# Attention of a two-layer hybrid block: how the low-rank heads' operands are split, and where their products stand between the attention units

## The chip, the cores and the metric

One core of one Trainium2 chip. The metric is the device time of one execution in microseconds, the median of the runs. Lower is better.

## What is computed

Two layers over 512 latent tokens (and 256 context tokens, 768 together), model width 1024. Each layer is half a SwiGLU, a token mixing, half a SwiGLU. The token mixing has grouped-query heads, a short convolution and low-rank heads side by side:

```python
def mla_heads(p, g_cq, g_ckv, w_uq, w_ukv, g_qn, g_kn, g_qr, g_kr):
    cq, ckv, kr = jnp.split(p, [MLA_Q_LORA, MLA_Q_LORA + MLA_KV_LORA], axis=-1)
    q = (rms_norm(cq, g_cq) @ w_uq).reshape(b, s, MLA_HEADS, MLA_NOPE + MLA_ROPE).transpose(0, 2, 1, 3)
    kv = (rms_norm(ckv, g_ckv) @ w_ukv).reshape(b, s, MLA_HEADS, MLA_NOPE + MLA_V).transpose(0, 2, 1, 3)
    ...
def token_mixing(...):
    ya_l, ya_c = gqa_mix(...)      # 6 query heads, 2 key heads, 64 wide
    ym_l, ym_c = mla_mix(...)      # 6 low-rank heads, 64 + 32 wide
    y_l = jnp.concatenate([ya_l, short_conv(s_l, conv_w, conv_b), ym_l], axis=-1) @ w_out
```

In layer 0 both latent and context tokens are queries (`need_ctx`); in layer 1 only the latent tokens are. Everything is float32.

## The kernel before

The kernel is written with a tile framework that tracks data and buffers; its compiler pass sets each engine's order of instructions from the program order, the dependencies and the free buffers. `chain("te")` holds TensorE to the written order in the attention. There ScalarE, VectorE and GpSimd have no such chain.

Nearly every float32 matrix product is done with split operands: x = hi + lo, where hi is x rounded to the fast format (`fp32r`) and lo is x - hi, and hi*hi, hi*lo and lo*hi are summed in PSUM.

**The attention** (`attend`) goes through a list of units. A unit is one head and two blocks of 128 queries. In layer 0 a head has three units, two with latent queries against 768 keys and one with the context queries against 256 keys, so units n = 2, 5, 8, ... are short; heads 0 to 5 are grouped-query heads and 6 to 11 the low-rank ones, so the low-rank units start at n = 18. In layer 1 a head has two units, and low-rank units start at n = 12. In step n TensorE does, in this order: the first scores of unit n; the first transposes of unit n-1's probabilities; then, if there is a "mid" job, the second transposes of n-1, the job, the second scores of n, and otherwise the second scores and then the second transposes; the third transposes of n-1; the "b" jobs; the values product of unit n-2; the "end" jobs. VectorE takes the row maxima, ScalarE the exponentials, and the transposed probabilities are split from PSUM by ScalarE (hi) and VectorE (lo).

PSUM has two score buffers of two banks (`ps`), shared by scores and by the products `uq` and `ukv`, and four one-bank buffers (`po`) for transposes and values products. Between a scores product and the reuse of its buffer stand the maxima and the exponentials.

**The jobs** make the later heads' operands while earlier heads are attended to:

- `uq(t)`: queries of the low-rank heads for token tile t (18 matmuls of 288 columns into a `ps` buffer; ScalarE copies and squares, VectorE sums the squares).
- `ukv(t)`: keys and values of token tile t (12 matmuls of 384 columns into a `ps` buffer; ScalarE copies, squares and scales, VectorE subtracts from PSUM for the lo part of the values, GpSimd copies the shared rope part).
- `load_ukv(hf)`: one half of the weights of `ukv`, loaded and split.
- `queries(p)`: two more grouped-query heads transposed and split into hi and lo.
- `q_norm`, `k_norm(t0, t1)`: norm factors, put as a list of small VectorE operations on `side`; `trickle()` takes two of them at each of six places in a step, `trickle(100)` takes all that are left. After the factors stand the scalings: GpSimd for the queries (with rope) and for key tiles 0 to 3, VectorE for key tiles 4 and 5.
- `mla_part(hd, which, t0)`: up to four token tiles of one head's query (`which` 0) or key (1), transposed by TensorE into a `po` buffer, scaled by ScalarE into a temporary y; after the last group VectorE casts y to hi and GpSimd subtracts (line 1862) for lo.
- `mixnorm_a`, `mixnorm_b`: two finished heads are divided by their row sums.

`at(n, place, f)` and `up_at(n, f, t)` put a job into step n. Layer 0's step 0 begins at 729.5 us of the profiled execution, step 5 at 770.3, step 8 at 792.2, step 12 at 810.5, step 16 at 830.2, step 18 at 843.9; in layer 1 step 0 begins at 2171.7, step 8 at 2229.2, step 12 at 2253.9, step 14 at 2264.7, step 18 at 2288.0.

Of the kernel before, what the change touches and what calls it, by code (L numbers as in the profile page):

```python
# [9 lines left out]
F32R = mybir.dt.float32r  # L10
I32 = mybir.dt.int32
AF = mybir.ActivationFunctionType
ALU = mybir.AluOpType
AX = mybir.AxisListType

P = 128
# [4 lines left out]
T = SEQ + CTX  # L21
# [20 lines left out]
LAG = 1  # L42
LATE = {0: 1, 2: 1, 4: 1, 6: 1}
NATIVE = (0, 2)


@with_exitstack
def tile_net(ctx: ExitStack, tc: tile.TileContext, a, out):
# [34 lines left out]
    te, ve, se, pe = Engine(nc.tensor, "te"), Engine(nc.vector, "ve"), Engine(nc.scalar, "se"), nc.gpsimd  # L83

    const = ctx.enter_context(tc.tile_pool(name="const", bufs=1))
    pool = ctx.enter_context(tc.tile_pool(name="pool", bufs=1))
# [4 lines left out]
    def nm(s):  # L91
        uid[0] += 1
        return f"{s}{uid[0]}"

    def slot(dt=F32, w=T):
        return pool.tile([P, w], dt, name=nm("s"), tag="s", bufs=NSLOT)

    def temp(dt=F32, w=T):
        return pool.tile([P, w], dt, name=nm("t"), tag="t", bufs=NTMP)
# [10 lines left out]
    def f32(t):  # L110
        return t.bitcast(F32)
# [1170 lines left out]
    def trickle(n=2):  # L1282

        for _ in range(n):
            if side:
                side.pop(0)()
# [154 lines left out]
    def mixing(l, hin, early, streams, nxt, pre):  # L1441
        h, E, accs = hin
        need_ctx = streams[-1][0].stop == T
# [8 lines left out]
        g96 = cst("g96", l, [96, 2])  # L1452
# [5 lines left out]
        mix = [None] * 8  # L1458
# [37 lines left out]
        for c0, w, nt in ((0, 384, nqt), (384, 288, NT)):  # L1496
# [5 lines left out]
            for t in range(nt):  # L1502
# [21 lines left out]
                lo = 0 if t < nqt else 384  # L1524
# [72 lines left out]
        stats = {"ckv": Stats(ALL, 2 * P), "cq": Stats(slice(0, wq), 3 * P)}  # L1597
# [14 lines left out]
        for i in range(5):  # L1612
            name, g, w = ("ckv", gckv[:, i:i + 1], T) if i < 2 else ("cq", gcq[:, i - 2:i - 1], wq)
# [87 lines left out]
        def uq(t, between=()):  # L1701
            q = slot()
            q_tok.append(q)
            sq = temp()
            pt = ps().rearrange("p (f c) -> p f c", f=2)
            up([pt[:, f, :288] for f in range(2)], t, comp["cq"], 288, wuq, between)
            se.copy(q[:, :576].rearrange("p (f c) -> p f c", f=2), pt[:, :, :288])
            se.activation(out=sq[:, :576].rearrange("p (f c) -> p f c", f=2), in_=pt[:, :, :288], func=AF.Square)
            sv = sq[:, :576].rearrange("p (h d) -> p h d", d=96)

            def sums():
                ve.tensor_reduce(out=st3[:, t, 0:6], in_=sv[:, :, 0:64], axis=AX.X, op=ALU.add)
                ve.tensor_reduce(out=st3[:, t, 6:12], in_=sv[:, :, 64:96], axis=AX.X, op=ALU.add)
            return sums
# [14 lines left out]
        def ukv(t):  # L1729
            pt = ps()  # L1730
            up([pt[:, 512 * f:512 * f + 384] for f in range(2)], t, comp["ckv"], 384, wukv)
            if t != spill:
                k_tok.append(slot())
            v = slot(F32R)
            VM.append(v)
            pv = pt.rearrange("p (f x) -> p f x", f=2)
            vv = v.rearrange("p (f h s d) -> p f h s d", f=2, s=2, d=64)
            rk = rr["ckv"][:, t:t + 1]
            vp = pv[:, :, 192:384].rearrange("p f (h d) -> p f h d", d=64)
            if t == spill:  # L1740
                srcs = (pt[:, 0:128], pt[:, 128:896].rearrange("p (a b) -> p a b", b=384)[:, :, 0:64], pt[:, 576:704])
                for (kv, hs), src in zip(heads_of(t), srcs):
                    se.copy(kv[:, :, 0:64], src if len(src.shape) == 3 else src.rearrange("p (h d) -> p h d", d=64))
            else:
                kv = k_tok[t][:, :576].rearrange("p (f h d) -> p f h d", f=2, d=96)
                se.copy(kv[:, :, :, 0:64], pv[:, :, 0:192].rearrange("p f (h d) -> p f h d", d=64))
            for kv, hs in heads_of(t):
                pe.tensor_copy(kv[:, :, 64:96], bc(krr[:, t, :], 1, hs.stop - hs.start))
            sq = temp()
            se.activation(out=sq[:, :384].rearrange("p (f c) -> p f c", f=2), in_=pv[:, :, 0:192], func=AF.Square)  # L1750
            se.mul(vv[:, :, :, 0, :], vp, rk)
            ve.scalar_tensor_tensor(out=vv[:, :, :, 1, :], in0=vp, scalar=rk, in1=f32(v).rearrange(
                "p (f h s d) -> p f h s d", f=2, s=2, d=64)[:, :, :, 0, :], op0=ALU.mult, op1=ALU.subtract)
            return lambda: ve.tensor_reduce(out=st3[:, t, 12:18], in_=sq[:, :384].rearrange("p (h d) -> p h d", d=64), axis=AX.X,
                                            op=ALU.add)
# [82 lines left out]
        mla, ys = {}, {}  # L1838
# [4 lines left out]
        def mla_part(hd, which, t0):  # L1843

            tok, n, w = ((query_of, nqt, wq), (key_of, NT, T))[which]
            if t0 == 0:
                ys[hd, which] = temp()
            y = ys[hd, which]
            tp = po()
            m = min(4, n - t0)  # L1850
            for t in range(m):
                te.transpose(out=tp[:96, t * P:(t + 1) * P], in_=tok(t0 + t, hd), identity=ident)
            se.mul(y[:96, t0 * P:(t0 + m) * P], tp[:96, :m * P], g96[:, which:which + 1])
            if t0 + m < n:
                return
            if which == 0:
                hi = pool.tile([P, T], F32R, name=nm("qh"), tag="wh", bufs=3)
                lo = pool.tile([P, T], F32R, name=nm("ql"), tag="wl", bufs=3)
            else:
                hi, lo = slot(F32R), slot(F32R)  # L1860
            ve.tensor_copy(hi[:96, :w], y[:96, :w])
            pe.tensor_sub(lo[:96, :w], y[:96, :w], f32(hi)[:96, :w])
            mla[hd, which] = hi[:96, :], lo[:96, :]

        def mla_unit(hd):
# [5 lines left out]
        def at(n, place, f, *args):  # L1871
            jobs.setdefault((n, place), []).append(lambda: f(*args))

        def up_at(n, f, t):
            def start():
                jobs.setdefault((n, "end"), []).insert(0, f(t))
            at(n, "mid", start)

        per = 3 if need_ctx else 2
        up_at(0, lambda t: uq(t, stats["cq"].count_steps(stats["cq"].acc)), 1)  # L1880
        at(0, "end", lambda: uq(2)())
        at(1, "b", lambda: stats["cq"].mean())
        up_at(1, uq, 3)
        if need_ctx:
            at(1, "end", lambda: uq(4)())
            at(1, "end", lambda: uq(5)())
        at(1, "end", load_ukv, 0)
        at(1, "end", load_ukv, 1)
        at(2, "end", queries, 1)
        at(2, "end", q_norm)  # L1890
        at(3, "end", queries, 2)
        for t, n in enumerate((4, 5, 6, 7, 9, 14) if need_ctx else (3, 4, 5, 6, 7, 8)):
            if t == 5 and need_ctx:
                at(n, "end", lambda: ukv(5)())
            else:
                up_at(n, ukv, t)
            if t == 3:
                at(n, "end", k_norm, 0, 4)
            elif t == 5:
                at(n, "end", k_norm, 4, 6)  # L1900
                at(n + 1, "b", trickle, 100)
        for hd in range(12):
            mk = (lambda hd=hd: gqa_unit(hd)) if hd < 6 else (lambda hd=hd: mla_unit(hd - 6))
            s = per * hd
            if 5 <= hd < 11:
                q, k = ((s - 1, s + 1) if hd == 5 else (s, s + 1)) if need_ctx else ((s - 1, s) if hd == 5 else (s, s))
                at(q, "b", mla_part, hd - 5, 0, 0)
                if nqt > 4:
                    at(q, "end", mla_part, hd - 5, 0, 4)
                at(k, "b" if k > q else "end", mla_part, hd - 5, 1, 0)  # L1910
                at(k, "end", mla_part, hd - 5, 1, 4)
            if hd >= 2 and hd % 2 == 0:
                i = hd // 2 - 1 if hd < 8 else hd // 2 + 1
                m = s + (2 if need_ctx else 1)
                at(m, "end", mixnorm_a, i)
                at(m + 1, "b", mixnorm_b, i, 0)
                if nqt > 4:
                    at(m + 1, "end", mixnorm_b, i, 4)
            for qbs in lat_units:
                units.append(Unit(qbs, ALL, list(range(NT)), mk))  # L1920
            if need_ctx:
                units.append(Unit((4, 5), CTXS, [4, 5], mk))
# [11 lines left out]
            nc.sync.dma_start(out=raw, in_=a["wo"][l, 0])  # L1934
            first_out.append(wsplit(raw, 1024))

        n0 = per * 11
        at(n0 - 1, "end", out_block)
        places = [(n0 + n, p) for n in range(4) for p in ("b", "end")]
        for i, (n, p) in zip((3, 4, 0, 1, 2, 5, 6), places):  # L1940
# [35 lines left out]
    def wm0_high(g):  # L1976
        if g in NATIVE:
            return
# [5 lines left out]
    def wm0_low(g, i):  # L1984
        if g in NATIVE:
            return
# [3 lines left out]
    def wm0_mm(g, k0=0, k1=KD):  # L1990
        if k0 == 0:
            pms[g] = ps()
        pm = pms[g]
        if g in NATIVE:
            for kk in range(k0, k1):
# [233 lines left out]
```

## Time and profile before

| | |
|---|---|
| median of 3 runs | 2744.41 us (2742.31 to 2748.45) |
| profiled execution, its own time | 2748.81 us |
| its span, first to last instruction | 2747.0 us |
| TensorE matmul busy | 2669.8 us, 97% |
| VectorE busy | 2038.7 us, 74% |
| ScalarE busy | 1145.5 us, 42% |
| GpSimd busy | 188.8 us, 7% |
| granted TensorE clock, mean | 0.993 |

The profile names an engine's instruction by its operation, the tile that it writes and those that it reads (`po<-ident,s`: a transpose into a `po` buffer), with the shapes. Nearly all VectorE, ScalarE and TensorE instructions pass through one helper and so have line 66; the tiles tell them apart: `t<-po,g` is `mla_part` on ScalarE, `qh<-t` its cast, `ql<-t,qh` and `s<-t,s` its subtraction on GpSimd. PE is TensorE, DVE is VectorE, ACT is ScalarE, POOL is GpSimd. In brackets behind a row stands how long the engine had been idle before it and which instruction ended that.

### The profile page before, as it was taken

The page shows a single profiled execution, that of the slowest core. Times are in us where ns is not written, and L with a number is a line of the kernel's source. Part 1 is how long each engine was busy: PE and PEld are TensorE (multiplying, and loading weights), DVE is VectorE, ACT ScalarE, POOL GpSimd, SP SyncE. Part 2 cuts the span into 40 slices and gives each one's busy share as a digit, 9 for nine tenths or more (in the row PEclk, how much of TensorE's full clock was granted, in tenths as well). Part 3 has the DMA queues.
Part 4 walks back from the last instruction along what each step waited for, and adds up shares of the span by engine and source line. Part 5 has one row for each costly group of instructions (what it writes and reads, how often), then busy time and mean ns, then how long its engine had stood idle before and what let it go on. Part 6 is the DMA issues. An engine that isn't in the chain of part 4 may idle for free. (4 is left out here: it accounts for less than half of the span.)

```text
span 2747.0 us, 40650 instructions
## 1 busy us (share of the span) xinstructions
PE 2669.8 (97%) x16088; PEld 2525.6 (92%) x16088; DVE 2038.7 (74%) x3475; ACT 1145.5 (42%) x1991; POOL 188.8 (7%) x248
## 2 busy tenths in 40 slices
PE   8999999999988999999999999999999999999999
PEld 5999999989888889999999999999998888888987
DVE  6856777777688887777777777777776788666655
ACT  5223333341477633333334433333343578444433
POOL 0000000001232200000000000000000233001110
PEclk9999999999999999999999999999999999999999
DMA  7313333233100321333333123333325101346543
GB/s 249 115 61 103 108 108 107 78 102 129 33 2 9 106 89 60 104 104 108 108 108 100 58 89 106 108 105 105 101 72 172 35 9 39 106 118 164 156 125 115
DMA packets 102927, 266.09 MB, mean 97 GB/s; under 512 B 12240, under 2 KB 41680, under 8 KB 102736
## 3 DMA queue, kind: packets, MB, share of 16 engines
q1 hardware_dynamic: 96112, 249.33, 27.4%
q0 software_dynamic: 6624, 14.16, 2.6%
q8 instruction: 127, 2.08, 0.3%
q14 instruction: 64, 0.52, 0.1%
HBM read 256.63 MB, written 2.10 MB: 94 GB/s over the span
## 5 line engine op out<-in xcount | busy, mean ns | idle before, releaser
L66 PE MATMUL ps<-s,wh 128*128 128x384 f32 (+2 forms) x4292 | 989.4, 340 | 6.9 <-ACT t L66 4.1
L66 PEld LDWEIGHTS ps<-s,wh 128*128 128x128 f32 x4292 | 743.6, 188 | 53.8 <-ACT t L66 5.2
L66 PE MATMUL po<-s,wh 128*128 128x384 f32 (+2 forms) x3164 | 768.6, 329 | 9.9 <-ACT t L66 9.3
L66 PE MATMUL ps<-s,wl 128*128 128x384 f32 (+2 forms) x2146 | 613.2, 338 | 0.9 <-DVE wl L66 0.8
L66 PEld LDWEIGHTS po<-s,wh 128*128 128x128 f32 x3164 | 553.2, 188 | 26.0 <-ACT t L66 12.4
L66 PE MATMUL po<-s,wl 128*128 128x384 f32 (+2 forms) x1582 | 519.2, 328 | 0.0
L66 PEld LDWEIGHTS ps<-s,wl 128*128 128x128 f32 x2146 | 387.0, 188 | 21.8 <-DVE wl L66 3.1
L66 PEld LDWEIGHTS po<-s,wl 128*128 128x128 f32 x1582 | 297.5, 188 | 6.2
L66 DVE SCALAR_TENSOR_TENSOR junk<-mr,sb 128x1024 fp8e4<-128x1024 f32 x224 | 273.7, 1222 | 14.4 <-DMA mr<-in_wm_dram 13.5
L66 DVE SCALAR_TENSOR_TENSOR xT<-ps,mod,xT 128x256 f32<-128x256 f32 (+1 forms) x360 | 198.7, 594 | 107.7 <-PE ps L66 105.9
L66 DVE TENSOR_TENSOR wl<-wr,wh 128x1024 fp32r<-128x1024 f32 (+3 forms) x179 | 192.2, 1076 | 114.5 <-ACT wh L66 114.3
L66 ACT CAST wh<-wr 128x1024 fp32r<-128x1024 f32 (+3 forms) x179 | 165.3, 927 | 203.1 <-PE ps L66 137.2
L66 ACT ACTIVATE t<-t 128x384 f32<-128x384 f32 (+1 forms) x142 | 70.9, 500 | 303.3 <-DVE t L66 303.3
L66 PE MATMUL po<-s,s 128*128 128x256 f32 (+3 forms) x1216 | 190.9, 307 | 6.0 <-DVE pl L66 2.0
L66 ACT COPY t<-po 128x384 f32<-128x384 f32 (+2 forms) x215 | 97.1, 452 | 225.1 <-PE po L66 223.1
L66 PEld LDWEIGHTS po<-s,s 128*128 128x128 f32 x1216 | 172.6, 189 | 13.3 <-DVE pl L66 2.5
L1526 POOL TENSOR_TENSOR t<-s 128x544 f32<-128x544 f32 (+1 forms) x12 | 13.0, 1095 | 1863.8 <-ACT s L66 1858.9
L66 DVE TENSOR_TENSOR s<-t,s 128x768 fp32r<-128x768 f32 (+3 forms) x144 | 104.3, 728 | 47.0 <-ACT s L66 46.4
L66 ACT CAST wh<-ws 128x1024 fp32r<-128x1024 f32 x71 | 74.8, 1054 | 146.5 <-PE ps L66 92.3
L66 ACT CAST s<-t 128x768 fp32r<-128x768 f32 (+3 forms) x144 | 92.9, 652 | 102.6 <-DVE t L66 102.5
L66 DVE TENSOR_TENSOR t<-po,t 128x384 f32<-128x384 f32 (+2 forms) x223 | 115.4, 523 | 27.3 <-ACT t L66 26.6
L66 PE MATMUL po<-s,w 128*128 128x384 f32 x636 | 119.9, 337 | 0.0
(198 smaller groups left out, 3413.0 us busy)
## 6 DMA issues: line engine op xcount, KB each, us to landing
mr<-in_wm_dram SPq DMA_DIRECT2D x128, 512.0 KB, 3.3
wr<-in_wg_dram SPq DMA_DIRECT2D x82, 512.0 KB, 3.2
wu<-in_wu_dram SPq DMA_DIRECT2D x71, 512.0 KB, 3.3
t<-in_wd_dram SPq DMA_DIRECT2D x80, 384.0 KB, 3.6
wr<-in_wiT_dram SPq DMA_DIRECT2D x22, 512.0 KB, 3.6
ws<-in_wu_dram POOLq DMA_DIRECT2D x36, 256.0 KB, 4.3
wr<-in_wu_dram SPq DMA_DIRECT2D x17, 512.0 KB, 3.3
wr<-in_wo_dram SPq DMA_DIRECT2D x14, 512.0 KB, 3.9
```

The lines of the kernel that those rows point to most:

```text
L66: f(*args, **kw)
L1526: pe.tensor_mul(sq[:, lo:544], x[:, lo:544], x[:, lo:544])
```

## The change

Two edits. The first is in `mla_part`: ScalarE writes the scaled group from PSUM as hi straight away, and VectorE makes lo from the same PSUM group; the temporary, VectorE's cast and GpSimd's subtraction are gone. For head 0 it also takes all that is left on `side` before its first group. The second puts the places of the jobs in a table `PLAN`, with other places than before:

| job | layer 0 before | layer 0 after | layer 1 before | layer 1 after |
|---|---|---|---|---|
| `uq` 3 | 1 mid | 1 mid | 1 mid | 1 end |
| `uq` 5 | 1 end | 2 mid | | |
| `queries` 1, 2 | 2, 3 end | 1, 5 end | 2, 3 end | 2, 4 end |
| `ukv` 0 to 5 | 4, 5, 6, 7, 9 mid, 14 end | 4 end, 5, 6, 8, 11, 12 mid | 3, 4, 5, 6, 7, 8 mid | 2 end, 4, 5, 7, 8, 8 mid |
| `k_norm` of tiles 0-3, 4-5 | 7, 14 end | 8, 12 end | 6, 8 end | 7, 8 end |
| all left on `side` | 15 b | 13 b | 9 b | 9 b |
| query, key of low-rank head 0 | 14, 16 | 13, 16 | 9, 10 | 9, 10 |
| query of heads 2, 4 | 21, 27 | 21, 27 | 14, 18 | 13, 17 |
| key of heads 2, 4 | 22, 28 | 22, 28 | 14, 18 end | 14, 18 b and end |

`uq` 1, 2 and 4, `load_ukv`, `q_norm`, the other heads' parts and `mixnorm` stay where they were.

```diff
         def mla_part(hd, which, t0):
 
             tok, n, w = ((query_of, nqt, wq), (key_of, NT, T))[which]
-            if t0 == 0:
-                ys[hd, which] = temp()
-            y = ys[hd, which]
+            if hd == 0:
+                trickle(100)
+            if t0 == 0 and which == 0:
+                ys[hd, which] = [pool.tile([P, T], F32R, name=nm("q" + p), tag="w" + p, bufs=3) for p in "hl"]
+            elif t0 == 0:
+                ys[hd, which] = slot(F32R), slot(F32R)
+            hi, lo = ys[hd, which]
             tp = po()
...
-            se.mul(y[:96, t0 * P:(t0 + m) * P], tp[:96, :m * P], g96[:, which:which + 1])
+            c, g = slice(t0 * P, (t0 + m) * P), g96[:, which:which + 1]
+            se.mul(hi[:96, c], tp[:96, :m * P], g)
+            ve.scalar_tensor_tensor(out=lo[:96, c], in0=tp[:96, :m * P], scalar=g, in1=f32(hi)[:96, c], op0=ALU.mult,
+                                    op1=ALU.subtract)
             if t0 + m < n:
                 return
-            if which == 0:
...
-            ve.tensor_copy(hi[:96, :w], y[:96, :w])
-            pe.tensor_sub(lo[:96, :w], y[:96, :w], f32(hi)[:96, :w])
...
+PLAN = {True: {'uq': [(0, 'mid'), (0, 'end'), (1, 'mid'), (1, 'end'), (2, 'mid')], 'load': 1, 'qs': (1, 5), 'qn': 2,
+  'ukv': [(4, 'end'), (5, 'mid'), (6, 'mid'), (8, 'mid'), (11, 'mid'), (12, 'mid')], 'first': (13, 16), 'even': (0, 1), 'odd': (0, 1), 'mix': 2, 'flush': None},
+  False: {'uq': [(0, 'mid'), (0, 'end'), (1, 'end')], 'load': 1, 'qs': (2, 4), 'qn': 2,
+  'ukv': [(2, 'end'), (4, 'mid'), (5, 'mid'), (7, 'mid'), (8, 'mid'), (8, 'mid')], 'first': (9, 10), 'even': (0, 0), 'odd': (-1, 0), 'mix': 1, 'flush': 9}}
...
+        for t, (n, p) in enumerate(plan["ukv"]):
+            place(n, p, ukv, t)
             if t == 3:
                 at(n, "end", k_norm, 0, 4)
             elif t == 5:
                 at(n, "end", k_norm, 4, 6)
-                at(n + 1, "b", trickle, 100)
+        if plan.get("flush") is not None:
+            at(plan["flush"], "b", trickle, 100)
```

More of the change, by code (lines that the diff above doesn't have):

```diff
@@ L44 @@
 NATIVE = (0, 2)
+PLAN = {True: {'uq': [(0, 'mid'), (0, 'end'), (1, 'mid'), (1, 'end'), (2, 'mid')], 'load': 1, 'qs': (1, 5), 'qn': 2, 'ukv': [(4, 'end'), (5, 'mid'), (6, 'mid'), (8, 'mid'), (11, 'mid'), (12, 'mid')], 'first': (13, 16), 'even': (0, 1), 'odd': (0, 1), 'mix': 2, 'flush': None}, False: {'uq': [(0, 'mid'), (0, 'end'), (1, 'end')], 'load': 1, 'qs': (2, 4), 'qn': 2, 'ukv': [(2, 'end'), (4, 'mid'), (5, 'mid'), (7, 'mid'), (8, 'mid'), (8, 'mid')], 'first': (9, 10), 'even': (0, 0), 'odd': (-1, 0), 'mix': 1, 'flush': 9}}
 @with_exitstack
@@ L1852, in mla_part @@
                 te.transpose(out=tp[:96, t * P:(t + 1) * P], in_=tok(t0 + t, hd), identity=ident)
-            se.mul(y[:96, t0 * P:(t0 + m) * P], tp[:96, :m * P], g96[:, which:which + 1])
+            c, g = slice(t0 * P, (t0 + m) * P), g96[:, which:which + 1]
+            se.mul(hi[:96, c], tp[:96, :m * P], g)
+            ve.scalar_tensor_tensor(out=lo[:96, c], in0=tp[:96, :m * P], scalar=g, in1=f32(hi)[:96, c], op0=ALU.mult,
+                                    op1=ALU.subtract)
             if t0 + m < n:
                 return
-            if which == 0:
[L1857 to L1860, printed above, removed]
-            ve.tensor_copy(hi[:96, :w], y[:96, :w])
-            pe.tensor_sub(lo[:96, :w], y[:96, :w], f32(hi)[:96, :w])
             mla[hd, which] = hi[:96, :], lo[:96, :]
@@ L1877, in up_at, with first, place @@
             at(n, "mid", start)
[L1879 to L1894, printed above, removed]
-            else:
-                up_at(n, ukv, t)
+        def first(hd):
+            return (3 if need_ctx else 2) * hd
+        plan = PLAN[need_ctx]
+        def place(n, p, f, t):
+            if p == "mid":
+                up_at(n, f, t)
+            else:
+                at(n, "end", lambda: f(t)())
+        for t, (n, p) in enumerate(plan["uq"]):
+            place(n, p, (lambda t: uq(t, stats["cq"].count_steps(stats["cq"].acc))) if t == 0 else uq, t + 1)
+        at(plan["uq"][0][0] + 1, "b", lambda: stats["cq"].mean())
+        at(plan["load"], "end", load_ukv, 0)
+        at(plan["load"], "end", load_ukv, 1)
+        for p, n in enumerate(plan["qs"]):
+            at(n, "end", queries, p + 1)
+        at(plan["qn"], "end", q_norm)
+        for t, (n, p) in enumerate(plan["ukv"]):
+            place(n, p, ukv, t)
             if t == 3:
@@ L1900, in mixing @@
                 at(n, "end", k_norm, 4, 6)
-                at(n + 1, "b", trickle, 100)
+        if plan.get("flush") is not None:
+            at(plan["flush"], "b", trickle, 100)
         for hd in range(12):
             mk = (lambda hd=hd: gqa_unit(hd)) if hd < 6 else (lambda hd=hd: mla_unit(hd - 6))
-            s = per * hd
+            s = first(hd)
             if 5 <= hd < 11:
-                q, k = ((s - 1, s + 1) if hd == 5 else (s, s + 1)) if need_ctx else ((s - 1, s) if hd == 5 else (s, s))
+                q, k = plan["first"] if hd == 5 else (s + d for d in plan["odd" if hd % 2 else "even"])
                 at(q, "b", mla_part, hd - 5, 0, 0)
@@ L1913, in mixing @@
                 i = hd // 2 - 1 if hd < 8 else hd // 2 + 1
-                m = s + (2 if need_ctx else 1)
+                m = s + plan["mix"]
                 at(m, "end", mixnorm_a, i)
@@ L1935, in out_block @@
             first_out.append(wsplit(raw, 1024))
-        n0 = per * 11
+        n0 = first(11)
         at(n0 - 1, "end", out_block)
```

## The prediction

> **What bounds the kernel now.** First the page: the span and the engines' shares.
>
> ```profile
> span 2747.0 us, 40650 instructions
> PE 2669.8 (97%) x16088; PEld 2525.6 (92%) x16088; DVE 2038.7 (74%) x3475; ACT 1145.5 (42%) x1991; POOL 188.8 (7%) x248
> ```
>
> TensorE bounds the kernel, and the change takes no matmul away. So it can win only TensorE's idle time and time at a low granted clock, and only in the attention. Second view: busy time by stretch, for the grouped-query and the low-rank part of layer 0 and the same two parts of layer 1.
>
> ```profile
> 724.00:845.00 121.00, 102.80 (x693) 95.83 (x692) 93.24 (x209) 85.68 (x194) 27.12 (x48) 0.93 0.02 7
> 845.00:934.00 89.00, 81.77 (x617) 75.56 (x616) 72.25 (x124) 77.66 (x174) 29.33 (x16) 1.00 0.06 19
> 2168.00:2246.00 78.00, 70.13 (x482) 65.17 (x480) 68.53 (x151) 59.64 (x127) 20.90 (x39) 0.98 0.03 8
> 2246.00:2326.00 80.00, 75.53 (x565) 70.00 (x564) 66.31 (x115) 67.21 (x145) 22.57 (x15) 1.00 0.06 20
> ```
>
> The columns are length, then PE, PEld, DVE, ACT and POOL busy, then the clock. TensorE is idle for 18.2, 7.2, 7.9 and 4.5 us, 37.8 us in all. VectorE is busy 77, 81, 88 and 83%: none of these stretches has one clear bound, a late VectorE instruction soon holds TensorE. Third view: TensorE's order of time, with the waits that the moved jobs touch.
>
> ```profile
> 754.18 0.39 PE L66 MATMUL ps<-k,s 128*128 128x256 f32 x1 [0.61 <-ACT t L66]
> 761.14 0.36 PE L66 MATMUL po<-ph,s 128*128 128x256 f32 x1 [1.42 <-DVE s L66]
> 770.26 0.39 PE L66 MATMUL ps<-k,s 128*128 128x256 f32 x1 [1.26 <-DVE s L66]
> 772.30 0.48 PE L66 MATMUL po<-ident,t 128*128 128x128 f32 x1 [1.42 <-ACT t L66]
> 792.15 0.35 PE L66 MATMUL ps<-k,s 128*128 128x256 f32 x1 [0.77 <-DVE s L66]
> 807.56 0.33 PE L66 MATMUL po<-ident,t 128*128 128x128 f32 x1 [1.68 <-ACT t L66]
> 827.40 0.50 PE L66 MATMUL ps<-s,s 128*128 128x512 f32 x1 [0.85 <-DVE s L66]
> 838.78 0.28 PE L66 MATMUL po<-ident,s 128*96 128x128 f32 x1 [3.11 <-DVE s L66]
> 2229.20 0.76 PE L66 MATMUL ps<-s,s 128*128 128x512 f32 x1 [2.12 <-DVE m L66]
> 2270.19 0.39 PE L66 MATMUL po<-s,s 128*128 128x256 f32 x1 [0.98 <-DVE pl L66]
> 2293.69 0.38 PE L66 MATMUL po<-s,s 128*128 128x256 f32 x1 [0.99 <-DVE pl L66]
> ```
>
> Last, the stretches around the three worst places, same columns.
>
> ```profile
> 768.00:780.00 12.00, 9.32 (x48) 8.85 (x47) 8.41 (x22) 6.56 (x17) 6.68 (x14) 0.72 0.00 1
> 834.00:843.00 9.00, 5.89 (x39) 5.70 (x38) 7.68 (x23) 6.57 (x17) 1.82 (x1) 0.83 0.17 55
> 2226.00:2236.00 10.00, 7.88 (x46) 7.42 (x45) 7.83 (x22) 4.74 (x11) 3.20 (x4) 0.83 0.01 2
> ```
>
> After such waits the clock falls. What that costs I take as the missing share of the clock times the busy time: 0.28 x 9.32 = 2.6 us, 0.17 x 5.89 = 1.0 us and 0.17 x 7.88 = 1.3 us.
>
> **The change, part by part.**
>
> *A. `uq` 5 to step 2 mid, first `queries` to step 1 end (layer 0).* The wait at 754.18 is for a score buffer that `uq` 5 had just filled; the one at 761.14 is a values product whose `po` buffer the split of the queries in step 2 still held. Both causes move: the query split runs one step earlier, where VectorE has no other backlog, and `uq` 5 stands between the two scores of a short unit, where its 18 matmuls cover the exponentials. Full value 2.03 us. The second half of the `ukv` weights reuses the buffer of `uq`'s weights, so its split now comes a step later; it is first needed by `ukv` 0 at the end of step 4, so I price that at nothing. I take -1.5.
>
> *B. `ukv` 0 to step 4 end, second `queries` to step 5 end.* The waits at 770.26 (a buffer that `ukv` 0 still held) and 772.30 (exponentials of step 4) come one behind the other at the start of step 5. At the end of step 4, `ukv` 0 stands just where the second wait was and covers it. But `ukv` 1 in step 5 then needs `ukv` 0's buffer sooner.
>
> ```profile
> L66 ACT COPY s<-ps 128x384 f32<-128x384 f32 x5 | 2.4, 482 | 4.8 <-PE ps L66 4.8
> L66 ACT ACTIVATE t<-ps 128x384 f32<-128x384 f32 x6 | 3.0, 502 | 0.0
> L66 ACT ACTIVATE s<-ps,m 128x384 fp32r<-128x384 f32 x6 | 3.5, 589 | 0.0
> L66 DVE SCALAR_TENSOR_TENSOR s<-ps,m,s 128x384 fp32r<-128x384 f32 x6 | 3.7, 612 | 0.0
> ```
>
> ```profile
> 780.85 0.60 PE L66 MATMUL po<-ident,t 128*128 128x128 f32 x4
> ```
>
> Emptying it takes 0.48 + 0.50 + 0.59 + 0.61 = 2.2 us; TensorE has only a short unit's first scores and eight transposes in between, some 1.2 us (twice the last row). So 1.0 us of wait returns, and with it I expect half of the clock loss (1.3). Full value 1.26 + 1.42 + 2.6 = 5.3; I take -3.0.
>
> *C. `ukv` 3 from step 7 to 8, `ukv` 4 from 9 to 11.* Step 7 has no cover any more, so step 8 starts as step 11 did before: 1.68 (807.56) in place of 0.77 (792.15), +0.9. Step 11 keeps its 1.68, as the job stands behind the first transposes there.
>
> *D. `ukv` 5 from step 14 to 12, first head's query from 14 to 13, all of `side` at 13.* The wait of 3.11 at 838.78 is the transposes of the first head's last key tiles, which VectorE had not scaled in time, and the one at 827.40 is for `ukv` 5's buffer. Both lose their cause: two to three steps lie between the scaling and its reader. The norm factors of `k_norm` now fall as a burst on step 13, before its maxima: 12 small operations of 0.16 and four scalings of 0.29 us, 3 us of VectorE, with the third transposes' splits queued behind:
>
> ```profile
> 836.84 0.16 DVE L66 SCALAR_TENSOR_TENSOR m<-m,m 128x12 f32<-128x12 f32 x1
> 838.08 1.17 DVE L66 TENSOR_TENSOR s<-s,m 128x384 f32<-128x384 f32 x4
> ```
>
> Full value 3.11 + 0.85 + 1.0 = 5.0; I take -4.0.
>
> *E. Layer 1: `ukv` one step later and the first `k_norm` from step 6 to 7.* The wait of 2.12 at 2229.20 has its root in a tiny operation:
>
> ```profile
> 2221.85 3.15 DVE L66 TENSOR_TENSOR m<-m 128x4 f32<-128x4 f32 x1
> 2224.06 0.94 POOL L1748 COPY s<-kr 128x192 f32<-128x192 f32 x3
> 2230.63 3.20 POOL L1797 TENSOR_TENSOR s<-s,m 128x384 f32<-128x384 f32 x4 [5.63 <-DVE m L66]
> ```
>
> The first `k_norm`'s opening product, 128x4, takes 3.15 us instead of some 0.16 (the row of 836.84), and ends when GpSimd's run of scalings and copies does, at 2225.0. One step later that run is over: -(2.12 + 1.3) = -3.4. [...] So I count 2.0 of it back and take -1.4. The other moves of `ukv` in layer 1 I set at zero: TensorE's 7.9 us of idle time in that stretch, less the 2.12, is spread over small waits, and two `ukv` in step 8 cover as much as they ask.
>
> *F. Layer 1: queries of heads 2 and 4 a step earlier.* At 2270.19 and 2293.69 (steps 14 and 18) transposes of `mixnorm` and of a query stand together ahead of the values product, and VectorE is late with the split. The query's four go to steps 13 and 17: full 1.97, I take -1.5.
>
> *G. `mla_part`.* Over both layers there are 24 head operands in 24 groups of 512 and 18 of 256 columns.
>
> ```profile
> L66 ACT ACTIVATE t<-po,g 96x512 f32<-96x512 f32 x24 | 16.6, 693 | 0.5
> L66 ACT ACTIVATE t<-po,g 96x256 f32<-96x256 f32 x18 | 8.5, 471 | 1.9 <-PE po L66 1.7
> L66 DVE CAST s<-t 96x768 fp32r<-96x768 f32 x12 | 6.7, 555 | 7.0 <-ACT t L66 7.0
> L1862 POOL TENSOR_TENSOR s<-t,s 96x768 fp32r<-96x768 f32 x12 | 22.1, 1838 | 44.6 <-DVE s L66 37.6 <-PE ps L66 5.0 <-PE po L66 2.1
> L1862 POOL TENSOR_TENSOR ql<-t,qh 96x512 fp32r<-96x512 f32 x6 | 7.7, 1284 | 44.0 <-DVE qh L66 35.5 <-DVE m L66 8.6
> L66 DVE TENSOR_TENSOR pl<-po,ph 128x512 fp32r<-128x512 f32 x74 | 49.5, 684 | 2.3 <-ACT ph L66 1.1
> L66 DVE TENSOR_TENSOR s<-po,s 128x256 fp32r<-128x256 f32 x50 | 19.0, 416 | 1.3 <-ACT s L66 1.3
> L66 DVE CAST qh<-t x12: 411/486/558, 828.1 to 2305.9; 96x768 fp32r<-96x768 f32 x6, 96x512 fp32r<-96x512 f32 x6
> ```
>
> ScalarE: the same 42 instructions with another output, 0. GpSimd loses 24 subtractions, 22.1 + 7.7 us and six more of 1.838, 41 us in all, that no TensorE wait in the four stretches names, so 0. VectorE loses 24 casts, 12 x 0.555 + 12 x 0.486 = 12.5 us, and gets 42 subtractions from PSUM, by the rows of the probabilities' split 24 x 0.684 + 18 x 0.416 = 23.9 us: +11.4 us. Also new: the `po` buffer is held past ScalarE until VectorE has come to it, and the next transposes but three need it. The waits of TensorE on VectorE in the two low-rank stretches stand today at:
>
> ```profile
> PE po L66 <- DVE s L66: 3.2, 4, 1.4
> PE po L66 <- DVE pl L66: 2.0, 2, 1.0
> ```
>
> The ends are 0 (all 30 us of VectorE's idle time there absorb it; a gain I exclude, as no wait names what goes) and +11.4 (none does). Nearest to these 5.2 us, with VectorE's share going from 82% to 89%, I take half as much again: +2.5.
>
> Sum: -1.5 - 3.0 + 0.9 - 4.0 - 1.4 - 1.5 + 2.5 = **-8.0 us**. Against the profiled execution, 2748.81 us (4.4 above the median of the runs), that is 2740.8; against the median, 2744.41, it is **2736.4**.
>
> **Rivals.**
>
> *1. The waits only move.* Units that lose a wait run into the next one, since maxima, exponentials and splits fill 71 to 88% of ScalarE and VectorE. The row at 807.56 speaks for it (a step without job waits 1.68), the double wait of step 5 against (both ends have a job's buffer as cause). Half of A to F returns: -5.3 + 2.5 = -2.8, 2741.6.
>
> *2. The clock does not depend on these waits.* [...] As a mechanism here: without the 1.3, 1.0 and 1.3 us counted in B, D and E (3.6), the sum is -4.4, 2740.0. Against it: the three falls stand exactly at the three largest sums of waits, 2.68, 3.11 and 2.12 us.
>
> *3. VectorE becomes the bound of the low-rank part (slower).* If the 11.4 us of G all show, and the gains of A to F halve, +6.1: 2750.5. It decides once VectorE passes TensorE in the stretch 845 to 934, that is 72.25 + 6 against 81.77 plus waits; that is still 4 us short, which speaks against it. The two waits of F, where the low-rank part already waits for VectorE's split, speak for it.
>
> **How the numbers follow.** Forecast 0.57, rival 1 0.18, rival 2 0.13, rival 3 0.12. 0.2% of the time, 5.5 us, is about what a measurement of this kernel can tell from no change. Faster: most of the forecast's cases and a few of rivals 1 and 2, 0.57; within: 0.32; slower: 0.11. With every full value and G at 0 the time is 2744.4 - 2.0 - 5.3 + 0.9 - 5.0 - 3.4 - 2.0 = 2727.6; the range goes a little beyond, for the waits that I set at zero, to 2725, and up to 2748, short of rival 3. The forecast's own range is 2727 to 2739.
>
> **What would show it.** A: no wait over 0.5 us between steps 2 and 3. B: one wait of about 1 us in step 5 and a clock above 0.8 around it. C: some 1.7 us at the start of steps 8 and 11. D: no wait above 1 us ahead of the first head's last key transposes in step 16. E: no VectorE product of 128x4 above 1 us, but perhaps one of 128x2. F: no wait on `pl` in steps 14 and 18. G: GpSimd's busy time down by 41 us, VectorE's up by 11, and TensorE's waits on VectorE in the low-rank stretches near 8 us. Wrong it is if these stretches, 368 us together, are not 5 us or more shorter, or if time changes outside the attention.

## The result and the profile after

| | before | after |
|---|---|---|
| median of 5 runs | 2744.41 us (2742.31 to 2748.45) | 2729.98 us (2728.24 to 2733.01) |
| ratio, 95% interval | | 0.995, 0.9934 to 0.9965 |
| span of the profiled execution | 2747.0 us | 2726.5 us |

The change makes the kernel 14.4 us faster; forecast were 8.0 us, 2736.4, with a range of 2725 to 2748. The page of the changed kernel, span and engines:

```profile
span 2726.5 us, 40636 instructions
PE 2661.4 (98%) x16088; PEld 2516.9 (92%) x16088; DVE 2046.0 (75%) x3493; ACT 1143.9 (42%) x1991; POOL 147.5 (5%) x224
```

TensorE has the same 16088 matmuls. GpSimd lost 41 us. To see where the time went, the attention is cut at the same instructions in both kernels: from the first scores of step 0 to the first scores with a low-rank query, and from there to the last transposes. Busy time by stretch of the kernel before, first the two grouped-query parts, then the low-rank ones:

```profile
729.54:843.85 114.31, 97.05 (x651) 90.46 (x650) 88.49 (x202) 80.00 (x184) 27.12 (x48) 0.93 0.02 6
2171.69:2253.86 82.17, 74.05 (x512) 68.68 (x511) 72.41 (x159) 61.83 (x133) 22.74 (x40) 0.98 0.02 4
843.85:933.59 89.74, 82.51 (x622) 76.21 (x621) 72.26 (x125) 77.62 (x174) 29.33 (x16) 1.00 0.05 17
2253.86:2328.70 74.84, 71.44 (x536) 66.40 (x535) 61.01 (x105) 64.06 (x139) 22.29 (x16) 1.00 0.08 33
```

The same stretches of the changed kernel:

```profile
727.96:830.71 102.75, 91.21 (x651) 84.14 (x649) 87.06 (x202) 79.95 (x184) 23.50 (x46) 1.00 0.02 4
2154.80:2233.58 78.78, 74.05 (x512) 68.78 (x511) 69.93 (x160) 62.16 (x134) 19.27 (x37) 0.98 0.01 4
830.71:919.59 88.88, 82.98 (x623) 76.39 (x621) 78.09 (x138) 77.83 (x177) 10.94 (x6) 1.00 0.06 21
2233.58:2307.84 74.26, 71.70 (x536) 66.39 (x535) 66.21 (x110) 63.48 (x139) 6.73 (x6) 1.00 0.08 31
```

The four parts are 11.6, 3.4, 0.9 and 0.6 us shorter, 16.4 us together. Length less busy time is TensorE's idle time: it fell from 17.3 to 11.5, from 8.1 to 4.7, from 7.2 to 5.9 and from 3.4 to 2.6, by 11.3 us. The other 5 us are busy time, nearly all of it in the first part, 97.05 against 91.21 us for the same 651 matmuls: there the clock was granted in full (1.00 against 0.93).

In part that is luck of two single executions. A second profile of the changed kernel, `after_again`, has the same idle time in this part, but again a low clock at step 0:

```profile
726.78:833.28 106.50, 95.03 (x650) 87.75 (x649) 87.11 (x202) 79.82 (x184) 23.44 (x46) 0.95 0.01 4
```

By that profile the first part is 7.8 us shorter, not 11.6. The remaining 4 us between the two spans lie outside the attention, where the code is the same, 2.9 of them between the two attentions (1238.1 and 1235.2 us). The prediction named time that changes outside the attention as a sign against it, and this is one; no run explains it. The profiled execution of before was itself 4.4 us above its median.

The waits behind it, in the changed kernel's order of time: in layer 0 those at the moved jobs and a new one in step 6, then the largest of layer 1:

```profile
754.48 0.33 PE L67 MATMUL po<-ident,t 128*128 128x128 f32 x1 [0.42 <-ACT t L67]
765.62 0.41 PE L67 MATMUL ps<-wh,s 128*128 128x384 f32 x1 [1.20 <-DVE m L67]
774.59 0.50 PE L67 MATMUL ps<-k,s 128*128 128x512 f32 x1 [0.73 <-ACT t L67]
782.55 0.33 PE L67 MATMUL po<-ident,t 128*128 128x128 f32 x1 [1.16 <-ACT t L67]
797.28 0.33 PE L67 MATMUL po<-ident,t 128*128 128x128 f32 x1 [1.76 <-ACT t L67]
813.09 0.29 PE L67 MATMUL po<-ident,s 128*96 128x128 f32 x1 [0.83 <-DVE m L67]
826.53 0.28 PE L67 MATMUL po<-ident,s 128*96 128x128 f32 x1 [0.54 <-DVE pl L67]
2179.20 0.47 PE L67 MATMUL ps<-k,s 128*128 128x512 f32 x1 [1.84 <-DVE s L67]
```

Row by row: A's waits of 2.03 us became 0.42 (and 0.62 in step 4); B's two became one of 1.20, ahead of `ukv` 1; two new ones stand in step 6 (0.73) and at the start of step 7 (0.44); steps 8 and 11 start with 1.16 and 1.76; D's 3.11 ahead of the first head's last keys is 0.54, with 0.83 for its query in step 13; and 1.84 in layer 1 is new.

### The profile page after: what moved, and what is told of

It reads as the page before. It is cut to its first block, busy times and chain, and to the rows that moved or that the text cites. A ratio compares the mean times of both kernels' runs of the same rounds, so it can differ in the third digit from the quotient of the medians.

```text
span 2726.5 us, 40636 instructions
## 1 busy us (share of the span) xinstructions
PE 2661.4 (98%) x16088; PEld 2516.9 (92%) x16088; DVE 2046.0 (75%) x3493; ACT 1143.9 (42%) x1991; POOL 147.5 (5%) x224
## 5 line engine op out<-in xcount | busy, mean ns | idle before, releaser
L67 PEld LDWEIGHTS po<-s,wh 128*128 128x128 f32 x3164 | 553.4, 188 | 26.0 <-ACT t L67 12.3
L67 DVE SCALAR_TENSOR_TENSOR junk<-mr,sb 128x1024 fp8e4<-128x1024 f32 x224 | 273.3, 1220 | 13.3 <-DMA mr<-in_wm_dram 12.2
L67 PEld LDWEIGHTS po<-s,s 128*128 128x128 f32 x1216 | 172.5, 189 | 12.2 <-DVE pl L67 2.4
L67 ACT CAST wh<-t 128x768 fp32r<-128x768 f32 x80 | 66.5, 835 | 115.4 <-PE ps L67 110.5
```

The source lines that it names most:

```text
L67: f(*args, **kw)
```

## The experiments

All ratios are to the kernel before, which was timed again beside each group of runs; its medians there were 2743.38, 2742.37 and 2743.80 us.

**The two edits apart.** `x1_split` has the first edit alone, `x2_table` the second alone (the old `mla_part`, with the emptying of `side` kept).

```diff
 x1_split: the new mla_part, PLAN with the places of the kernel before, side emptied there
 x2_table: PLAN as changed, in mla_part:
+            y = temp()
+            se.mul(y[...], tp[...], g96[...]); ve.tensor_copy(hi, y); pe.tensor_sub(lo, y, hi)
```

> Only the first edit: hi by ScalarE and lo by VectorE straight from PSUM, all jobs at their old places. Theory (the table brings the gain, the split only loads VectorE): the grouped-query parts keep their length (114 and 82 us), the low-rank parts get 1 to 3 us longer together, the time is 2744 to 2747 us. [...]

> Only the second edit: all jobs at the places of the table, with the old split (temporary, VectorE's cast, GpSimd's subtraction). Theory (the table brings the gain): 2729 to 2732 us, the grouped-query parts 103 and 79 us as in the changed kernel. Rival (the split brings a part): 2733 to 2738 us, and the wait of TensorE on VectorE stays where GpSimd subtracts.

Measured: the split alone 2742.61 us, 0.9995 (0.9982 to 1.0008); the table alone 2731.23 us, 0.9957 (0.9942 to 0.9972). The table makes the gain; what the split does to the whole cannot be told from nothing. In its low-rank parts it costs nothing, though:

```profile
836.74:925.43 88.69, 83.17 (x623) 76.64 (x622) 77.29 (x136) 77.53 (x175) 10.95 (x6) 1.00 0.05 17
2245.56:2320.05 74.49, 71.78 (x537) 66.69 (x536) 65.93 (x110) 63.92 (x140) 6.99 (x6) 1.00 0.09 32
```

Against before (89.74 and 74.84 us) they are 1.1 and 0.4 us shorter, with VectorE 5 us busier in each. The theory's half about the table holds; its half about the split, 1 to 3 us longer, falls. The rival of `x2_table`, 2733 to 2738 us, is too high as well. One sign of it did come: with the table alone layer 0's low-rank part keeps its length (89.93 us), and TensorE's waits on VectorE stay there (3.1 us, 3.2 before).

The lengths forecast for the first grouped-query part, 114 us with the split alone and 103 with the table alone, were both missed:

```profile
728.22:836.74 108.52, 92.17 (x651) 85.45 (x649) 89.04 (x204) 80.18 (x184) 23.43 (x46) 0.98 0.02 6
727.89:835.22 107.33, 94.99 (x650) 87.67 (x649) 87.25 (x199) 79.67 (x183) 27.11 (x48) 0.95 0.01 4
```

With the split alone every wait of steps 0 to 5 is where it was, yet 4.9 us of busy time are gone, as the clock fell only once in this part (0.98 against 0.93). So the lengths of this part in two profiles say little; its idle times say more: 17.3 before, 16.4 with the split alone, 12.3 with the table alone. Over all four parts idle time fell by 3.9 us with the split alone and by 9.2 with the table alone.

**The table by parts.** `x3_d_e` moves only D in layer 0 and only the first `k_norm` in layer 1, `x4_a_b_f` only A and B, and F; both with the old split.

```diff
 x3_d_e, on the kernel before:
-ukv 5 at (14, end), head 0's query at 14, side emptied at (15, b); layer 1: k_norm(0, 4) at 6
+ukv 5 at (12, mid), head 0's query at 13, side emptied at (13, b); layer 1: k_norm(0, 4) at 7
 x4_a_b_f, on the kernel before:
-uq 5 at (1, end), queries at 2 and 3, ukv 0 at (4, mid); layer 1: queries of heads 2, 4 at 14, 18
+uq 5 at (2, mid), queries at 1 and 5, ukv 0 at (4, end); layer 1: queries of heads 2, 4 at 13, 17
```

> The kernel before with D alone in layer 0 (ukv 5 in step 12, first head's query and the rest of the side list in step 13) and E alone in layer 1 (the first k_norm put at the end of step 7 instead of 6, every ukv where it was). Theory (each wait has its job as cause, full value): the wait of 3.11 ahead of the first head's key transposes falls below 1, layer 0's grouped-query part gets 5 us shorter; in layer 1 no 128x4 product takes over 0.3 us, its grouped-query part gets 3.4 us shorter; the time is 2735 to 2737 us. Rival (waits only move): half of that, 2740 us, with new waits above 1 us within the next two steps.

> The kernel before with A and B alone in layer 0 (uq 5 in step 2, queries in steps 1 and 5, ukv 0 at the end of step 4) and F alone in layer 1 (queries of heads 2 and 4 a step earlier). Theory: the waits at the starts of steps 3 and 5 fall from 4.7 to 1 us together and the clock stays at 1.0 there, layer 0's grouped-query part gets 6 us shorter, layer 1's low-rank part 2 us, the time is 2736 to 2738 us. Rival (the falls of the clock do not depend on these waits): the clock still falls to 0.6 to 0.8 in a stretch of 10 us around step 5 or step 0, and the part gets only 3 us shorter.

Measured: 2738.06 us, 0.9978 (0.9966 to 0.999), and 2736.42 us, 0.9972 (0.9961 to 0.9983). The two together, 5.3 + 7.0 = 12.3 us, are the table's 12.2, though each is good to some 3 us only. In `x3_d_e` the wait of 3.11 is gone, and the largest within the steps around it is 0.69; its 128x4 product takes 0.15 us (both rows from its order of time):

```profile
815.83 0.29 PE L67 MATMUL po<-ident,s 128*96 128x128 f32 x1 [0.69 <-ACT t L67]
2213.83 0.15 DVE L67 TENSOR_TENSOR m<-m 128x4 f32<-128x4 f32 x1
```

In `x4_a_b_f` the waits of steps 3 to 7 are those of the changed kernel: 0.42, 0.64, 1.20, 0.68 and 0.44. The forecast of 1 us of returned wait ahead of `ukv` 1 was good, but the others were not named. The first grouped-query part of each:

```profile
729.27:834.44 105.17, 91.61 (x650) 84.00 (x649) 87.83 (x199) 80.08 (x183) 27.11 (x48) 1.00 0.01 4
728.97:836.79 107.82, 92.11 (x650) 85.47 (x649) 88.57 (x202) 80.00 (x184) 27.16 (x48) 0.98 0.02 6
```

They are 9.1 and 6.5 us shorter, where 5 and 6 were expected. Idle time fell from 17.3 to 13.6 us with D, near the full value of its waits: there the rival, in which the waits only move, falls. With A and B it fell only to 15.7, by 1.6 us of their 4.7: there most of the waiting did move. The rest of the shorter lengths is busy time, as neither execution had a low clock at steps 0 and 5; step 0's waits are untouched in both, so its part is luck. What did not come as expected is layer 1 of `x3_d_e`: TensorE's idle time fell from 8.1 to 6.2 us there, but the part was only 0.7 us shorter instead of 3.4, as the clock fell in it at another place.

**GpSimd's run.** `x5_less_gpsimd` is the kernel before, with less work for GpSimd in layer 1. It leaves out the scaling and the rope of two query tiles, so it computes something else and only its trace is used.

```diff
-            for t in range(nqt):
+            for t in range(nqt if need_ctx else 2):
                 side.append(lambda t=t: scale(t))
```

> The kernel before; in layer 1 GpSimd leaves out the norm scaling and rope of the low-rank queries of token tiles 2 and 3, so its run of scalings ends some 8 us sooner; everything else stands where it stood. [...]

Measured, in its order of time (VectorE, GpSimd):

```profile
2218.16 0.15 DVE L67 TENSOR_TENSOR m<-m 128x4 f32<-128x4 f32 x1
2216.21 0.65 POOL L1749 COPY s<-kr 128x192 f32<-128x192 f32 x2 [2.76 <-PE po L67]
```

With GpSimd's run over at 2216.9, the product takes 0.15 us in place of 3.15, and no wait above 0.32 us is left at the start of step 8, where 2.12 was. Both the length and the wait came from the run of GpSimd, and not from a VectorE that is simply behind in that step; how the run holds the product up is not shown. The time, 2738.84 us, is a single one. In `x4_a_b_f`, where layer 1 is unchanged up to step 12, VectorE came to the product at the same place of GpSimd's run, 3.2 us ahead of its end:

```profile
2213.34 1.49 DVE L67 TENSOR_TENSOR m<-m 128x4 f32<-128x4 f32 x1
2215.08 0.92 DVE L67 SCALAR_TENSOR_TENSOR m<-st,m 128x24 f32<-128x24 f32 x1
```

Here the product took 1.49 us and ended 1.7 us before the run did (2216.5). The next small operation then took 0.92 us instead of 0.16, and the wait at step 8 was still 1.94.

**The clock.** `x6_fill` puts matmuls into the longest wait.

```diff
+        def fill():
+            t = po()
+            for _ in range(11):
+                te.matmul(out=t, lhsT=qst[0][:, 0:P], rhs=kst[0][0][:, 0:512], start=True, stop=True)
+        if need_ctx:
+            at(16, "end", fill)
```

> The kernel before with 11 matmuls of 512 columns, whose product is not read, put into TensorE's wait of 3.1 us ahead of the first head's last key transposes (layer 0, step 16). They take some 2.5 us and end before the wait does. Theory (the clock falls because TensorE idles there): the clock stays at 1.0 in the stretch behind it, the matmuls of layer 0's grouped-query part take 1.5 us less, the end of the wait stays where it was. Rival (the fall has nothing to do with the wait): the clock still falls to 0.7 to 0.85 in the 9 us behind it, in this run as in the three that had this wait.

The 12 us from some 2 us ahead of the end of that wait, the wait unfilled in the kernel before, in `x1_split`, `x4_a_b_f` and `x5_less_gpsimd`, and filled in `x6_fill`:

```profile
837.00:849.00 12.00, 10.22 (x67) 9.89 (x68) 8.02 (x18) 7.26 (x20) 1.82 (x1) 0.86 0.14 45
```

```profile
830.00:842.00 12.00, 10.36 (x67) 10.03 (x68) 9.27 (x21) 7.37 (x19) 0.00 (x0) 0.86 0.13 45
```

```profile
830.00:842.00 12.00, 10.27 (x67) 9.94 (x68) 7.98 (x18) 7.23 (x19) 1.81 (x1) 0.86 0.15 45
```

```profile
833.00:845.00 12.00, 9.73 (x55) 9.49 (x56) 8.32 (x20) 6.37 (x17) 1.82 (x1) 0.72 0.14 45
```

```profile
831.00:843.00 12.00, 11.38 (x82) 10.39 (x81) 10.38 (x26) 8.48 (x23) 1.84 (x1) 1.00 0.14 45
```

Four of four with the wait lose clock there, the filled one does not, and neither do the seven profiles of kernels in which D's moves have taken the wait away. The theory holds for this wait. The whole is slower: 2749.12 us, 1.0022 (1.0006 to 1.0038). Its profile shows the extra time behind the second attention: from 2310 us on TensorE's waits above 0.8 us add up to 14.4 us, against 7.9 in the kernel before. Why is not explained.

**Two more places.** `v1_ukv0_mid` and `v2_ukv3_end` change one place each in the changed kernel.

```diff
 v1_ukv0_mid, layer 1:
-'ukv': [(2, 'end'), ...]
+'ukv': [(3, 'mid'), ...]
 v2_ukv3_end, layer 0:
-'ukv': [..., (8, 'mid'), (11, 'mid'), (12, 'mid')]
+'ukv': [..., (7, 'end'), (11, 'mid'), (12, 'mid')]
```

> The changed kernel with ukv 0 of layer 1 back in step 3 mid (from step 2 end). Theory (the wait of 1.84 us ahead of step 3's second scores is for the score buffer that ukv 0 still holds, since nothing stands between them): that wait falls below 0.5, the idle time of layer 1's grouped-query part falls from 4.3 to 2.5 us, the time is 2 us under the changed kernel's (0.993 of before). Rival (the buffer is waited for one place later instead): a wait of 1 us or more at the start of step 3 or 4, time as the changed kernel's (0.995).

> The changed kernel with ukv 3 of layer 0 at the end of step 7 (from step 8 mid). Theory (a product at the end of a long step covers the exponentials that the next, short step waits for, but its buffer is then asked for by the short step's second scores): the wait of 1.16 us at the start of step 8 goes and one of 1 to 2 us comes ahead of step 8's second scores; time within 1 us of the changed kernel's. Rival (only the cover counts): the idle time of layer 0's grouped-query part falls by 1 us or more with no new wait above 0.5.

`v1_ukv0_mid`: 2731.11 us, 0.9956 (0.9938 to 0.9973). The wait of 1.84 is gone, one of 0.74 for exponentials came at the start of step 3, and layer 1's grouped-query part is 76.56 us long, with 3.8 us of idle time against 4.7 in the changed kernel. The theory is right about the buffer; its gain of 2 us in the whole does not show. `v2_ukv3_end`: 2733.54 us, 0.9964 (0.9952 to 0.9976); in its order of time, step 8's second scores:

```profile
789.27 0.35 PE L67 MATMUL ps<-k,s 128*128 128x256 f32 x1 [2.24 <-DVE m L67]
```

The product covers the exponentials, and the short step then pays 2.24 us for the buffer in place of 1.16: the theory's mechanism, a little dearer than it said. Its median is 3 us above the changed kernel's, with intervals that overlap. A last pair was timed on one chip:

> The changed kernel once more, on the chip and in the rounds of the next one. Both theories: 0.993 to 0.9965 of before. Theory (a wait of 1.6 us or more throws the clock back only in some executions): the waits at the same places as in its first profile, to 0.1 us, while the stretches of low clock are others.

> ukv 0 of layer 1 in step 3 mid, beside the changed kernel. Theory (its wait of 1.84 us is gone, 1.3 us of idle time net, and with it a possible low stretch of the clock worth 1.7 us): 1 to 3 us under the changed kernel. Rival (no more than the noise): within 1 us of it.

Measured: the changed kernel 2730.72 us, 0.9951 (0.9934 to 0.9968), and `v1_again` 2724.19 us, 0.9929 (0.9909 to 0.9949). The theory about the clock holds: the waits of the changed kernel are those of its first profile to within 0.1 us, but its low clock is now at step 0 and not behind the 1.84 of layer 1, where the first profile had it. Of `v1_again` the median is 6.5 us lower, but the intervals overlap, and the same kernel had 0.9956 in its first comparison; its idle time in the part is 0.8 to 0.9 us less in both profiles. It is the better version by the trace, and not shown to be so by the times.

## Why the prediction was right, and where its sizes were off

The direction, the range and the place were right: the gain is in the attention, in layer 0's grouped-query part above all, and came from the table. The forecast was 6 us short, and its 8.0 lies outside the interval of the gain, 9.6 to 18.1 us.

- **A to F** were right in sum. The prediction took -10.5; the table alone gave -12.2, with an interval from -15.9 to -7.7. D and E were to give 5.4 and gave 5.3, A, B and F 6.0 and 7.0. But the sum holds errors that cancel. A and B named one return (1.20 against 1.0), and more came: only 1.6 of their 4.7 us of idle time were gained, and in the profile of `x4_a_b_f` most of the rest is busy time, that is the clock. D had no return worth 1 us, though VectorE's burst did fall on step 13. For E the 2.0 us counted back are a term that no run shows: the changed kernel has no VectorE product of 128x4 or 128x2 above 0.3 us, and in `x3_d_e` one of 128x2 took 0.63 us instead of 0.15, while GpSimd's four scalings ran. A return of another kind came, at a move set at zero: `ukv` 0 at the end of step 2, 1.84 us, since nothing stands in step 3 between it and the second scores that need its buffer. The moves set at zero also took away waits that the prediction did not name (1.09, 0.57 and 0.87 us ahead of step 6), so that the part's idle time fell by 3.4 us in all.
- **C** was right in step 11 (1.76 against 1.68) and too dear in step 8 (1.16).
- **F** is not the earlier queries' alone. The waits on the split in steps 14 and 18 of layer 1 fall to 0.4 with the split of G alone as well as with the earlier queries alone.
- **G had the wrong sign, and this is the step that failed.** +2.5 was taken for the whole; the split alone gave -0.8, with an interval from -4.9 to +2.2, and the low-rank parts got 1.1 and 0.4 us shorter. TensorE's waits on VectorE there, forecast near 8 us, went from 5.2 to 4.2 in the changed kernel. The price of VectorE's work was even low: its 42 subtractions took

```profile
L67 DVE SCALAR_TENSOR_TENSOR s<-po,g,s 96x512 fp32r<-96x512 f32 x12 | 8.9, 742 | 0.7 <-ACT s L67 0.7
L67 DVE SCALAR_TENSOR_TENSOR ql<-po,g,qh 96x512 fp32r<-96x512 f32 x12 | 8.8, 734 | 0.0
L67 DVE SCALAR_TENSOR_TENSOR s<-po,g,s 96x256 fp32r<-96x256 f32 x12 | 5.7, 477 | 0.7 <-ACT s L67 0.4
L67 DVE SCALAR_TENSOR_TENSOR ql<-po,g,qh 96x256 fp32r<-96x256 f32 x6 | 2.9, 479 | 1.9 <-ACT qh L67 1.8
```

  26.3 us instead of 23.9, as the form with a scalar takes some 0.06 us more than the plain subtraction (96 partitions here, 128 there). VectorE's idle time took it all. What failed is "a gain I exclude, as no wait names what goes". The kernel before, VectorE, GpSimd and TensorE in layer 0's low-rank part, and then the same VectorE operation in `x1_split`:

```profile
907.38 2.20 DVE L66 TENSOR_TENSOR wl<-wo,wh 128x1024 fp32r<-128x1024 f32 x1
906.67 1.83 POOL L1862 TENSOR_TENSOR ql<-t,qh 96x768 fp32r<-96x768 f32 x1 [6.66 <-DVE qh L66]
910.24 0.38 PE L66 MATMUL po<-ph,s 128*128 128x256 f32 x1 [1.43 <-DVE s L66]
```

```profile
897.79 1.23 DVE L67 TENSOR_TENSOR wl<-wo,wh 128x1024 fp32r<-128x1024 f32 x1 [0.19 <-ACT wh L67]
```

  VectorE's subtraction for the weights' lo part starts while GpSimd subtracts, and takes 2.20 us instead of 1.23. The split behind it, for which TensorE then waits 1.43 us, is late by that; the wait names VectorE and not GpSimd. All six kernels with GpSimd's subtraction have this operation at 2.20 or 2.21 us and a wait of 1.43 to 1.46 behind it; the six without it have 1.22 or 1.23 and no wait above 0.4 at that product, though in the changed kernel 0.73 us come 1.5 us behind it instead (897.00). With the split alone TensorE's waits for VectorE's `s` fell from 3.2 to 2.2 us in this part, 1.0 of the 1.7 us of idle time that it lost. For layer 1 the same is not shown: why its waits of 0.98 and 0.99 fall to 0.45 and 0.44, by GpSimd or by a buffer's or a temporary's earlier release, no run separates.
- **The clock terms.** The falls do go with the waits, against rival 2, but not each time. In five profiles with B's double wait of 1.26 and 1.42 the clock fell twice; step 0, whose waits (0.94, 0.68 and 1.62) no kernel here touches, had a fall in five of twelve. The kernel before had such a fall at step 0 in its profile, which the prediction did not price, and the changed one had not: 2.5 us of busy time in steps 0 to 2 (25.0 against 22.5), and no work of the change. B's fall was priced too low: the prediction multiplied the missing share with the busy time, 0.28 x 9.32 = 2.6; with the length of the stretch it is 0.28 x 12 = 3.4, and the busy time of steps 3 to 5 fell by 3.2 us (18.4 against 15.2).

Rival 1 (the waits only move) falls in its time, half of A to F, with `x2_table`; as a mechanism it falls for D and is largely right for A and B. Rival 3 (VectorE becomes the bound) falls with `x1_split`.

## What to carry to other kernels

Where two engines besides the bound one are 80% busy, price a wait by its cause. Here a wait for an operand that was made too late (D) went nearly as a whole once its job stood earlier, while waits for a product's buffer and for exponentials (A and B) came back by two thirds, in the same steps and the next ones. A product put behind a long step covers the exponentials, and the next short step then waits for its buffer (2.24 us in `v2_ukv3_end`) unless something stands in between. What an engine loses to a neighbour need not appear as a wait that names the neighbour: look for one instruction far longer than others of its form (2.20 against 1.23 us here). And where the clock falls in some executions only, as at step 0 in five of twelve profiles, compare idle time between single profiles, not length.

## What of the hardware was not expected

In the kernel before a VectorE operation on 128x4 elements took 3.15 us, twenty times the 0.15 of `x5_less_gpsimd`, while GpSimd ran one tensor operation after another. Three times (3.15, and 3.11 in `x1_split` and `x6_fill`) it ended with GpSimd's run of 16 us; in `x4_a_b_f` it ended after 1.49 us with 1.7 us of the run to go, so there it did not have to wait for the run's end.

The clock fell to half, and in nearly equal portions. In slices of 1 us it is 0.50 where it is lowest, in the kernel before (840 to 843 us, behind the wait of 3.11) as in the changed one (2181 to 2183 us, behind 1.84). Over 12 us the clock was 0.86 after the 3.1 us wait in three kernels and 0.72 in a fourth, that is 0.14 x 12 = 1.7 us of full speed, or twice that; the five falls at step 0, summed in the same way over stretches of 4 us, come to 1.7, 3.4 (twice) and 5.1 us (twice). Why in portions is not shown.

The waits that a fall goes with are of many lengths. Those of 3.1 us had one behind them in four of four, those of 1.94 to 2.13 in three of four, of 1.83 or 1.84 in two of four, and step 0 with waits of 0.94, 0.68 and 1.62 within 11 us in five of twelve; in the kernel before the clock is at 0.50 there from 734.5 us on, ahead of the 1.62 (736.4 to 738.0). In `x3_d_e` it fell between 2226 and 2238 us (0.76 and 0.67 in slices of 6 us), where no wait is above 0.83. But the one of 2.24 in `v2_ukv3_end` was followed by no fall, and those of 1.68 and 1.76 at step 11 by none in eleven profiles, so length alone does not tell it.
